# RWKV's output projection in a two-layer hybrid trunk: its first two tiles issued as a pair

## The chip, the core and the metric

The kernel runs on one core of one Trainium2 chip. The metric is the device time of one execution in microseconds (us). Before the change it is 2279.49 us, the median of 3 runs that lay between 2275.8 and 2281.12 us.

## What is computed

Each of two layers mixes 512 tokens of 1024 channels in two ways, gates both and adds them up; a feed-forward block (FFN) with a short convolution and a small gated embedding follow.

```python
y_att = sliding_window_attention(q, k, v, att_sinks) @ w_o_att
y_rw = rwkv7_time_mix(rw, ...) @ w_o_rw                      # the projection that the change touches
mixed = sigmoid(gate_a) * y_att + sigmoid(gate_b) * y_rw
x = x + rmsnorm(mixed @ w_out)
h = rmsnorm(x)
ua, ub = split(causal_dwconv3(h @ w_up))                     # 2816 + 2816 channels
x = x + rmsnorm((gelu(ua) * ub) @ w_down)
x = x + rmsnorm(sigmoid(x @ w_ple_gate) * (p[i] @ w_ple))
```

Everything is in 32-bit floats.

## The kernel before

**Layout.** Activations lie transposed: a tensor of 1024 channels is eight tiles of 128 channels x 512 tokens. A weight matrix is cut into output tiles `m` of 128 columns; each is loaded in two halves of four 128-row blocks (`w`, 128x512, 256 KB).

**A matmul in three.** To keep 32-bit accuracy, every operand is split in two parts: a rounded high part and the rest. ScalarE (ACT) writes the high part (`wh` of a weight, `yr` or `hh` of an activation), then VectorE (DVE) subtracts to get the low part (`wl`, `hl`; for `yr` both parts bear that name). `mm3` (lines 251 to 256) then issues three TensorE (PE) matmuls per block `k`: line 254 high x high, line 255 the low part of the activation, line 256 the low part of the weight. An output tile of 1024 input channels takes 8 x 3 = 24 matmuls.

**Accumulators (PSUM banks).** `PM(cls)` (line 102) hands out the bank in which an output tile is summed. There are two banks named `pm` and one named `pf`. With class "x" a counter `self.nx` goes round the three: m, m, f, m, m, f, ... (line 104). With class "m" or "f" the bank is named by the caller and the counter stays where it is. A bank is used again only when the instruction that reads its sum has finished; the scheduler puts a wait on the first matmul of the next tile in it.

**Weight buffers.** `load_w` (line 136) has classes too: "m" has 2 raw buffers `w` and 3 each of `wh` and `wl`; "f" has 1 and 2 and 2. Class "x" alternates between them by a counter of its own, `self.nw`; `proj` (line 258) loads an output tile's two halves so, one in each class, and issues its 24 matmuls.

**Who sets the order.** The kernel is written in program order, but a scheduler reorders each engine's instructions by priority and by its own idea of when operands are ready. Each engine then runs its list strictly in that order. All data transfers are issued by one queue (SP) in order too.

**Around the change.** The recurrence of RWKV runs in four groups (`rwkv`, line 572); group g writes rows 2g and 2g+1 of the scratch tensor `yrd`. The next work in the program is the gate of the RWKV branch (`gate`, line 835), the attention's output projection (`att_out`, line 510, weights `w_oa`, evacuated by DVE as `ta`), and then the part that the change edits (lines 921 to 942): eight loads `yr <- yrd` of 128x512, each split into the two parts; then for each of eight output tiles m a projection by `w_or[l, m]`, and its evacuation `tb <- tb, p` (which frees the bank), `+ mt`, and a split into `hh`, `hl`. The scratch buffers of `ta`, `yr`, `tb` and `mt` come from one pool of three (`F`, line 847), so that the fourth load of `yr` has to wait until an earlier buffer has been split.

**After it.** The same class "x" counter is used by the projections that come later: `w_out` (`lin`, line 949), the FFN's up projection (`ffn`, line 1096), its down projection and the embedding's gate. In between some tiles name their bank. In the FFN, `conv(m)` (line 1099) runs for the pairs (0, 22), (1, 23), (2, 24), (3, 25) and so on (FT = 22). The first five tiles were computed ahead; tile 3 is taken in bank `pf` and tile 24 in a bank `pm`, by name (line 1101); tile 25 is the first that takes a bank from the counter. What frees a bank here is DVE's `un <- p, rs` (line 1107), followed by two convolution steps `cv` (lines 1109, 1110).

Of the kernel before, what the change touches and what calls it, by code (L numbers as in the profile page):

```python
# [19 lines left out]
P = 128  # L20
T = 512
DM = 1024
KT = DM // P
# [32 lines left out]
class Trunk:  # L56
# [291 lines left out]
    @staticmethod  # L348
    def row(t, k):
        return t[k * P:(k + 1) * P, :]  # L350
# [491 lines left out]
    def run(self):  # L842
        nc, tc, a = self.nc, self.tc, self.a
# [22 lines left out]
        for l in range(self.L):  # L866
# [54 lines left out]
            yact = []  # L921
# [10 lines left out]
                yact.append(self.split(t, hi, lo))  # L932
            self.cls = "x"
            mixed = []
            for m in range(KT):
                ps = self.proj(a["w_or"][l, m], yact)
                tb, mt = F("tb"), F("mt")
                self.dma(tb, row(self.tbd, m))
                self.dma(mt, row(self.mad, m))
                self.stt(tb, tb, 1.0, ps, ALU.add, ALU.mult)  # L940
                self.tt(tb, tb, mt, ALU.add)
                mixed.append(self.split(tb, *hb[m]))
# [68 lines left out]
            for m in range(KT):  # L1011
# [3 lines left out]
                ps = self.PM("f") if m % 2 else self.PT("ple")  # L1015
# [189 lines left out]
```

## Time and profile before

| | us |
|---|---|
| three timed runs: median (lowest, highest) | 2279.49 (2275.8, 2281.12) |
| the profiled execution, own time | 2275.79 |
| its span, first to last instruction | 2274.1 |
| PE busy | 2192.8 (96% of the span) |
| DVE busy | 1544.7 (68%) |
| ACT busy | 1120.0 (49%) |
| mean granted TensorE clock | 0.993 |

The profile is of one execution. All places in time below are microseconds from the start of its span. A timeline row reads: start, duration, engine, line, operation, output <- inputs, shapes, count; in brackets the idle time of the engine before it and what ended that. A matmul's duration covers its way through the array; what a matmul costs in a stream is the distance from its start to the next one's start. Timeline rows leave out the buffer numbers, the rows of the program's order keep them.

### The profile page before, as it was taken

The numbers are of one execution on the slowest core, as the hardware profiler recorded it, in microseconds if no ns is written. First come the engines' busy times: TensorE is split into PE (matmuls) and PEld (weight loads), VectorE is DVE, ScalarE is ACT, GpSimd is POOL, SyncE is SP. The second block draws the span as 40 slices with busy tenths as digits, with TensorE's granted clock in tenths as the row PEclk, the third lists the DMA queues.
The fourth block names the chain that finished last, engine by engine and source line by source line (L and its number), as shares of the span: only waits on it lengthen the run. The fifth ranks groups of instructions, "written<-read, shape, count | busy, mean of one in ns | idle before, by whom it ended". The sixth has DMA issues, their size and how long they took to land. (4 is left out here: it accounts for less than half of the span.)

```text
span 2274.1 us, 39486 instructions
## 1 busy us (share of the span) xinstructions
PE 2192.8 (96%) x14340; PEld 1730.1 (76%) x14340; DVE 1544.7 (68%) x3683; ACT 1120.0 (49%) x2450; POOL 26.7 (1%) x86
## 2 busy tenths in 40 slices
PE   7999999999999999999999999999999999999996
PEld 6766776667689788888896677766677888888886
DVE  6864689777666877733877647789666668776356
ACT  4566445555444654432445655556443545454332
POOL 1000000000000000000000000000000000000000
PEclk9999999999999999999999999999999999999998
DMA  4522333355571433343235233333456623333431
GB/s 154 172 91 93 104 92 88 85 145 176 178 247 31 134 98 98 95 121 114 83 128 154 86 123 96 82 96 103 124 168 208 214 75 102 98 98 98 123 106 60
DMA packets 204515, 269.40 MB, mean 118 GB/s; under 512 B 71840, under 2 KB 84640, under 8 KB 204320
## 3 DMA queue, kind: packets, MB, share of 16 engines
q1 hardware_dynamic: 204320, 266.88, 38.7%
q8 instruction: 113, 1.85, 0.3%
q14 instruction: 82, 0.67, 0.1%
HBM read 218.95 MB, written 42.47 MB: 115 GB/s over the span
## 5 line engine op out<-in xcount | busy, mean ns | idle before, releaser
L125 ACT ACTIVATE wh<-w 128x512 fp32r<-128x512 f32 (+1 forms) x590 | 352.9, 605 | 514.5 <-PE pm L255 173.3
L159 DVE TENSOR_TENSOR wl<-w,wh 128x512 fp32r<-128x512 f32 (+2 forms) x574 | 376.7, 661 | 263.9 <-ACT wh L125 243.7
L254 PE MATMUL pm<-hh,wh 128*128 128x512 f32 x1040 | 421.1, 405 | 1.9 <-ACT wh L125 1.2
L256 PE MATMUL pm<-hh,wl 128*128 128x512 f32 x1040 | 419.4, 403 | 2.7 <-DVE wl L159 2.7
L255 PE MATMUL pm<-hl,wh 128*128 128x512 f32 x1040 | 415.3, 399 | 0.0
L254 PEld LDWEIGHTS pm<-hh,wh 128*128 128x128 f32 x1040 | 195.4, 188 | 51.3 <-issue 7.0
L256 PEld LDWEIGHTS pm<-hh,wl 128*128 128x128 f32 x1040 | 195.5, 188 | 48.4 <-DVE wl L159 4.3
L255 PEld LDWEIGHTS pm<-hl,wh 128*128 128x128 f32 x1040 | 195.3, 188 | 41.5 <-issue 2.4
L254 PE MATMUL pf<-hh,wh 128*128 128x512 f32 x512 | 205.5, 401 | 5.4 <-ACT hh L125 2.4
L256 PE MATMUL pf<-hh,wl 128*128 128x512 f32 x512 | 204.0, 398 | 0.0
L255 PE MATMUL pf<-hl,wh 128*128 128x512 f32 x512 | 203.2, 397 | 0.5 <-DVE hl L128 0.5
L134 DVE SCALAR_TENSOR_TENSOR cv<-un,vec,cv 128x510 f32<-128x510 f32 (+1 forms) x176 | 130.8, 749 | 23.2 <-ACT cv L125 20.6
L254 PEld LDWEIGHTS pf<-hh,wh 128*128 128x128 f32 x512 | 96.4, 188 | 33.9 <-ACT gt L125 4.8
L256 PEld LDWEIGHTS pf<-hh,wl 128*128 128x128 f32 x512 | 96.7, 189 | 23.3 <-issue 2.3
L255 PEld LDWEIGHTS pf<-hl,wh 128*128 128x128 f32 x512 | 96.7, 189 | 21.0 <-DVE hl L128 1.2
L254 PE MATMUL pm<-uh,wh 128*128 128x512 f32 (+1 forms) x248 | 89.3, 360 | 2.0 <-ACT wh L125 2.0
L256 PE MATMUL pm<-uh,wl 128*128 128x512 f32 (+1 forms) x248 | 89.4, 361 | 0.0
L255 PE MATMUL pm<-ul,wh 128*128 128x512 f32 (+1 forms) x248 | 88.9, 359 | 0.0
L125 ACT ACTIVATE cv<-un,vec 128x512 f32<-128x512 f32 x88 | 71.2, 814 | 28.3 <-DVE un L128 28.2
L128 DVE TENSOR_TENSOR acc<-acc,sq 128x256 f32<-128x256 f32 (+1 forms) x114 | 49.9, 462 | 38.5 <-ACT sq L125 38.0
L128 DVE TENSOR_TENSOR un<-pm,rs 128x512 f32<-128x512 f32 x56 | 38.5, 690 | 39.8 <-PE pm L256 39.8
L703 DVE TENSOR_TENSOR Z<-Z 128x126 f32<-128x126 f32 (+22 forms) x248 | 62.0, 250 | 3.7
(409 smaller groups left out, 4440.5 us busy)
## 6 DMA issues: line engine op xcount, KB each, us to landing
w<-in_w_up_dram SPq DMA_DIRECT2D x156, 256.0 KB
w<-in_w_dn_dram SPq DMA_DIRECT2D x80, 256.0 KB
w<-in_w_q_dram SPq DMA_DIRECT2D x32, 256.0 KB
w<-in_w_ga_dram SPq DMA_DIRECT2D x32, 256.0 KB
w<-in_w_k_dram SPq DMA_DIRECT2D x32, 256.0 KB
w<-in_w_r_dram SPq DMA_DIRECT2D x32, 256.0 KB
w<-in_w_v_dram SPq DMA_DIRECT2D x32, 256.0 KB
w<-in_w_gb_dram SPq DMA_DIRECT2D x32, 256.0 KB
```

The source lines that it names most:

```text
L125: return self.nc.scalar.activation(out=out, in_=in_, func=func, **kw)
L128: return self.nc.vector.tensor_tensor(out=out, in0=in0, in1=in1, op=op)
L134: return self.nc.vector.scalar_tensor_tensor(out=out, in0=in0, scalar=s, in1=in1, op0=op0, op1=op1)
L159: self.nc.vector.tensor_tensor(out=wl, in0=w, in1=wh.bitcast(F32), op=ALU.subtract)
L254: mm(ps, wh, ah, start=start, stop=False)
L255: mm(ps, wh, al, start=False, stop=False)
L256: return mm(ps, wl, ah, start=False, stop=stop).ins
L703: nc.vector.tensor_tensor(out=zt[:, :n, jj + 1:], in0=zt[:, :n, jj + 1:], in1=tv, op=ALU.add)
```

## The change

The first two output tiles of the projection, m = 0 and m = 1, are no longer done by `proj` one after the other. Tile 0 gets a bank `pm` and both its weight halves in class "m", tile 1 gets bank `pf` and both halves in class "f". Their matmuls are written as: blocks 0 to 5 of tile 0, blocks 0 to 5 of tile 1, then blocks 6 and 7 (the rows of the recurrence's last group) of tile 0 and of tile 1. The evacuations and tiles 2 to 7 are as before. Since the two tiles name their banks, the counter `nx` moves six steps in this loop, not eight; `nw` moves twelve, not sixteen.

```diff
             self.cls = "x"
             mixed = []
+            pair = [(self.PM(c), self.whole(a["w_or"][l, i], P, c)) for i, c in enumerate("mf")]
+
+            for ks in (range(6), range(6, KT)):
+                for ps, ws in pair:
+                    for k in ks:
+                        self.mm3(ps, ws[k], yact[k], k == 0, k == KT - 1)
             for m in range(KT):
-                ps = self.proj(a["w_or"][l, m], yact)
+                ps = pair[m][0] if m < 2 else self.proj(a["w_or"][l, m], yact)
                 tb, mt = F("tb"), F("mt")
                 self.dma(tb, row(self.tbd, m))
                 self.dma(mt, row(self.mad, m))
```

What the scheduler makes of it, at three places.

**PE, layer 0, the first matmuls of the projection.** `yr_6909`/`yr_6910` are the two parts of block 0, `yr_6915`/`yr_6916` those of block 1. Before, `pm_6953` is tile 0 and `pm_6998` tile 1:

```order
L254 MATMUL pm_6953<-yr_6909,wh_6956 128x512
L255 MATMUL pm_6953<-yr_6910,wh_6956 128x512
L256 MATMUL pm_6953<-yr_6909,wl_6958 128x512
L254 MATMUL pm_6953<-yr_6915,wh_6956 128x512
L254 MATMUL pm_6998<-yr_6909,wh_7001 128x512
L255 MATMUL pm_6998<-yr_6910,wh_7001 128x512
L256 MATMUL pm_6998<-yr_6909,wl_7003 128x512
L255 MATMUL pm_6953<-yr_6916,wh_6956 128x512
```

After, tile 1 is `pf_6966`:

```order
L254 MATMUL pm_6953<-yr_6909,wh_6956 128x512
L255 MATMUL pm_6953<-yr_6910,wh_6956 128x512
L256 MATMUL pm_6953<-yr_6909,wl_6958 128x512
L254 MATMUL pm_6953<-yr_6915,wh_6956 128x512
L254 MATMUL pf_6966<-yr_6909,wh_6969 128x512
L255 MATMUL pf_6966<-yr_6910,wh_6969 128x512
L256 MATMUL pf_6966<-yr_6909,wl_6971 128x512
L255 MATMUL pm_6953<-yr_6916,wh_6956 128x512
```

Nothing has moved: the scheduler interleaved tiles 0 and 1 already. Of the rest of the two tiles only two matmuls have moved: the second and third of tile 1's block 5 stand ahead of tile 0's block 6 now, no longer among its block 7. Tile 1's bank is another.

**PE, layer 0, the start of the FFN's up projection.** `pm_8470` is tile 24, `pf_8507` tile 3, and the last name tile 25, the first whose bank comes from the counter. Before:

```order
L255 MATMUL pm_8470<-hl_116,wh_8380 128x512
L256 MATMUL pm_8470<-hh_115,wl_8382 128x512
L256 MATMUL pf_8507<-hh_115,wl_8394 128x512
L254 MATMUL pm_8538<-hh_101,wh_8541 128x512
L255 MATMUL pm_8538<-hl_102,wh_8541 128x512
L256 MATMUL pm_8538<-hh_101,wl_8543 128x512
```

After:

```order
L255 MATMUL pm_8470<-hl_116,wh_8380 128x512
L256 MATMUL pm_8470<-hh_115,wl_8382 128x512
L256 MATMUL pf_8507<-hh_115,wl_8394 128x512
L254 MATMUL pf_8538<-hh_101,wh_8541 128x512
L255 MATMUL pf_8538<-hl_102,wh_8541 128x512
L256 MATMUL pf_8538<-hh_101,wl_8543 128x512
```

No row has moved. Tile 25 is in bank `pf` now, the one that the row just ahead of it has filled for tile 3. DVE's list, from the start of this FFN to `un <- pf_8507`, is the same in both kernels. In layer 1 the counter has been shifted twice, and tile 25 is in a bank `pm` before and after.

**SP, layer 1, the transfers around the load of block 1 (`yr_18754`).** `w_18858` and `w_18814` are the second half of tile 1's weights, `w_18975` a half of tile 4's, `mad` a store, `yr_18760` block 2. Before:

```order
L122 DMA yrd1_12444<-yo_18045 128x512
L122 DMA g_18058<-gd1_12879 128x512
L122 DMA mad1_18419<-ta_18666 128x512
L122 DMA yr_18754<-yrd1_12444 128x512
L122 DMA w_18858<-in_w_or_dram 128x512
L122 DMA w_18975<-in_w_or_dram 128x512
L122 DMA yrd1_12444<-yo_18059 128x512
L122 DMA yr_18760<-yrd1_12444 128x512
```

After:

```order
L122 DMA yrd1_12444<-yo_18045 128x512
L122 DMA g_18058<-gd1_12879 128x512
L122 DMA w_18814<-in_w_or_dram 128x512
L122 DMA mad1_18419<-ta_18666 128x512
L122 DMA yr_18754<-yrd1_12444 128x512
L122 DMA w_18975<-in_w_or_dram 128x512
L122 DMA yrd1_12444<-yo_18059 128x512
L122 DMA yr_18760<-yrd1_12444 128x512
```

The weight half has moved from two places behind the store to the place ahead of it, so that it is now ahead of block 1's load. ACT and DVE likewise split this weight half ahead of block 1, and no longer behind it. On PE in layer 1 four matmuls (block 0 of tile 1, and the first of tile 2) have moved ahead of the first one that needs block 1, and tile 3 has bank `pf`, which was tile 1's.

## The prediction

> **What bounds the kernel now.** I read the page's busy shares first, then PE's timeline where the edited projection runs, then every later place where the bank counter matters.
>
> ```profile
> span 2274.1 us, 39486 instructions
> PE 2192.8 (96%) x14340; PEld 1730.1 (76%) x14340; DVE 1544.7 (68%) x3683; ACT 1120.0 (49%) x2450; POOL 26.7 (1%) x86
> ```
>
> PE is the bound: it stands still for 81 us of 2274. An edit of order can win only out of those 81 us, and whatever makes PE wait at a place where it does not wait now is paid in full, as long as PE stays busy behind it. In the projection PE waits once in each layer. PE's timeline, layer 0 and then layer 1:
>
> ```profile
> 609.37 0.39 PE L256 MATMUL pm<-yr,wl 128*128 128x512 f32 x1
> 612.79 1.11 PE L254 MATMUL pm<-yr,wh 128*128 128x512 f32 x2 [3.03 <-ACT yr L125]
> ...
> 1730.49 0.39 PE L256 MATMUL pm<-yr,wl 128*128 128x512 f32 x1
> 1733.10 0.73 PE L254 MATMUL pm<-yr,wh 128*128 128x512 f32 x2 [2.23 <-ACT yr L125]
> ```
>
> The waits of 3.03 and 2.23 us are not for the last group's rows. In the order of the program the first instruction behind the 3.03 us wait needs block 3 and the one behind the 2.23 us wait needs block 1; both are rows of early groups, and what is late is their load and split. These places are all that the edit aims at. With the clock (below) they are worth at most 3.03 + 1.7 + 2.23 = 7 us.
>
> **The projection, layer 0: nothing to gain.** PE's list had the two tiles interleaved already, and SP's, ACT's and DVE's lists are the same up to block 4, weights by other names aside. So the 3.03 us wait for block 3 comes again. What can be new is that tile 1 now sums in bank `pf`, which the last tile of the attention's projection has just used. DVE's row that frees it, then PE's first rows that would need it:
>
> ```profile
> 605.42 0.69 DVE L134 SCALAR_TENSOR_TENSOR ta<-ta,pf 128x512 f32<-128x512 f32 x1 [0.29 <-PE pf L256]
> ...
> 606.04 0.72 PE L254 MATMUL pm<-yr,wh 128*128 128x512 f32 x2
> 606.61 0.40 PE L255 MATMUL pm<-yr,wh 128*128 128x512 f32 x1
> ```
>
> The bank is free at 605.42 + 0.69 = 606.11. The second of the two merged matmuls is tile 1's first, 0.23 ahead of 606.61, at 606.38: 0.27 us to spare. Were it late by some tenths, the wait for block 3 behind it would take that up. The weight splits that ACT and DVE have ahead of block 5 now are covered by PE's matmuls on blocks 3 and 4. Layer 0's projection: 0, bounds -0.2 and +0.5.
>
> **The FFN's start, layer 0: a new wait.** Tile 25 moves to bank `pf`, whose last matmul for tile 3 is the row just ahead of it. So PE cannot go on before DVE has run `un <- pf` for tile 3. PE's timeline there:
>
> ```profile
> 757.35 0.39 PE L256 MATMUL pf<-hh,wl 128*128 128x512 f32 x1
> 757.57 0.39 PE L254 MATMUL pm<-hh,wh 128*128 128x512 f32 x1
> 757.80 0.39 PE L255 MATMUL pm<-hl,wh 128*128 128x512 f32 x1
> 758.75 0.50 PE L256 MATMUL pm<-hh,wl 128*128 128x512 f32 x1 [0.56 <-DVE wl L159]
> 759.08 0.40 PE L254 MATMUL pm<-hh,wh 128*128 128x512 f32 x1
> ```
>
> And DVE's:
>
> ```profile
> 757.35 0.75 DVE L134 SCALAR_TENSOR_TENSOR cv<-un,vec,cv 128x510 f32<-128x510 f32 x1
> 758.01 0.69 DVE L159 TENSOR_TENSOR wl<-w,wh 128x512 fp32r<-128x512 f32 x1
> 758.61 0.68 DVE L128 TENSOR_TENSOR ul<-cv,uh 128x512 fp32r<-128x512 f32 x1
> 759.21 0.69 DVE L159 TENSOR_TENSOR wl<-w,wh 128x512 fp32r<-128x512 f32 x1
> 759.81 0.68 DVE L128 TENSOR_TENSOR un<-pm,rs 128x512 f32<-128x512 f32 x1
> 760.41 0.68 DVE L159 TENSOR_TENSOR wl<-w,wh 128x512 fp32r<-128x512 f32 x1
> 761.01 0.68 DVE L128 TENSOR_TENSOR un<-pf,rs 128x512 f32<-128x512 f32 x1
> ```
>
> Before, tile 25 starts at 757.57, stands 0.7 us for its low weight, and its fourth matmul is at 759.08. DVE has no idle in its rows: it is behind here, and its list is the same after the change, so `un <- pf` ends at 761.01 + 0.68 = 761.69 as before. From a DVE result to the PE matmul that waits for it, the rows give 758.75 - (758.01 + 0.69) = 0.05. Tile 25 starts at 761.74; the first matmul after a wait costs 0.33 (758.75 to 759.08), the next ones 0.23, so its fourth is at 761.74 + 0.33 + 2 x 0.23 = 762.53. **Delay: 762.53 - 759.08 = 3.45 us.** The 0.7 us wait for the low weight is inside it, since that is ready at 758.70. Bounds 3.0 and 3.8, if DVE runs half a step (0.6 us) earlier or later. The next tiles 4, 26 and 5 have banks that are free by then, and their weights are split by DVE ahead of or soon after this, so nothing is won back: PE has no wait over 0.5 us in the rest of this FFN.
>
> **The clock behind that wait.** PE's granted clock falls to a half for 3.41 us at a time. Five stretches of that length, from the answer by windows (from:to, length, PE busy and matmuls, weight loads, DVE, ACT, POOL, granted clock, DMA):
>
> ```profile
> 609.52:612.94 3.42, 0.39 (x3) 0.15 (x2) 1.56 (x3) 0.83 (x2) 0.00 (x0) 1.00 0.91 348
> 612.94:616.35 3.41, 3.41 (x9) 2.50 (x10) 2.36 (x4) 1.69 (x3) 0.00 (x0) 0.50 0.84 252
> 616.35:619.76 3.41, 3.41 (x17) 2.81 (x16) 1.92 (x4) 1.87 (x3) 0.00 (x0) 1.00 0.70 201
> 1210.27:1213.68 3.41, 1.99 (x7) 0.78 (x5) 3.36 (x8) 2.05 (x4) 0.00 (x0) 1.00 0.79 274
> 1213.68:1217.10 3.42, 3.26 (x8) 2.40 (x8) 3.33 (x9) 1.83 (x5) 0.00 (x0) 0.50 0.81 275
> 1729.09:1732.51 3.42, 1.79 (x8) 1.13 (x7) 1.98 (x3) 0.87 (x2) 0.00 (x0) 1.00 0.92 319
> 1732.51:1735.92 3.41, 2.82 (x12) 2.36 (x13) 1.38 (x2) 1.31 (x3) 0.00 (x0) 1.00 0.95 281
> ```
>
> A full stretch holds some 15 matmuls of 512 columns. Stretches with 3 and with 7 were followed by one at half clock, the stretch with 8 was not: the line lies near half. A slow stretch filled with work loses half of 3.41, 1.7 us. The new wait lasts from 757.57 to 761.74, 4.17 us, so at least one stretch is less than half filled, wherever the borders fall. How much is lost hangs on them: if the slow stretch lies partly on the wait itself, 0.5 to 1.3; one full stretch, 1.7; if that is thin too and a second one follows, up to 2.6. I take 1.6, near the middle and near the one full stretch that the 3.03 us wait cost.
>
> The Trainium skill (TensorE: Matmul & The Clock Gate, "Why this matters for your kernels") puts the line elsewhere: no PE gaps over some 3 us, since a whole idle window sends the clock back. This trace disagrees at 1213.68, where a stretch with 7 matmuls was enough; what a rule of whole stretches would give is the first rival.
>
> **The projection, layer 1: about nothing.** SP has the second half of tile 1's weights ahead of the load of block 1 now. ACT's rows for block 1, that weight, and block 2; PE's first matmul on block 2; and SP's issues:
>
> ```profile
> 1732.42 0.63 ACT L125 ACTIVATE yr<-yr 128x512 fp32r<-128x512 f32 x1 [2.09 <-DMA yr<-yrd]
> 1733.17 0.64 ACT L125 ACTIVATE wh<-w 128x512 fp32r<-128x512 f32 x1
> 1735.79 0.63 ACT L125 ACTIVATE yr<-yr 128x512 fp32r<-128x512 f32 x1 [1.98 <-DMA yr<-yrd]
> ...
> 1736.47 0.73 PE L254 MATMUL pm<-yr,wh 128*128 128x512 f32 x2
> ...
> 1728.12 0.38 SPq L122 DMA_DIRECT2D yr<-yrd  x1
> 1728.55 0.99 SPq L122 DMA_DIRECT2D w<-in_w_or_dram  x2
> ```
>
> Block 1 and this weight half change places in the queue, so block 1 should be ready when the weight was: some 0.7 us later (1733.17 against 1732.42). PE has four matmuls (0.9 us) more to do ahead of it, and ten instead of fourteen behind it until it needs block 2, which was ready at 1736.42 and was needed at 1736.47. So the same work is done when block 2 comes. Block 3 takes the buffer that block 1 frees, so its load may go out 0.7 us later: at most +0.7, below nothing not more than -0.2. Further on, tile 3 shares tile 1's bank, which by DVE's list is freed about when PE gets there: 0 to +0.5. I take +0.3 for layer 1, bounds -0.2 and +1.2; it is nearer to nothing since the load of block 2 is not moved.
>
> **Sum.** 0 + 3.45 + 1.6 + 0.3 = +5.35 us: 2275.79 + 5.35 = 2281.1 in the profiled execution's own time. That execution lies 3.7 us below the median of the runs, so the median comes to 2279.5 + 5.35 = **2284.8 us**, 0.23% slower. About 0.2% (4.6 us) is what a measurement of this kernel can tell from no change.
>
> **The rivals.**
>
> *The clock holds.* If only a stretch without any matmul lowers it, the 4.17 us wait covers a whole stretch in (4.17 - 3.41) / 3.41 = 22% of positions; in the others the sum is 3.45 + 0.3 = +3.75: 2283.2, within 0.2%. For it: the 2.23 us wait of layer 1 cost no clock. Against: 1213.68. Chance 0.14.
>
> *Not slower: the waits for `yr` are filled.* If the paired order lets the loads of the blocks come sooner (the weight halves of tile 1 in the other class leave SP's queue earlier), both waits go, -7, and the FFN's wait remains: 5.05 - 7 = -1.9: 2277.6. It decides in whether block 3 is split before 609.6 in layer 0, 3 us sooner than now. Against: SP's list up to that load is the same. Chance 0.06.
>
> *Next to nothing happens.* The scheduler had done the interleaving itself, and DVE frees `pf` in time. For that it would have to be 4.1 us ahead of these rows; it has no idle to draw that from. +0.3: 2279.8. Chance 0.10.
>
> *Slower still.* All upper bounds meet: 3.8 + 2.6 + 1.2 + 0.5 = +8.1: 2287.6. Chance 0.08.
>
> The forecast keeps 0.62.
>
> **How the numbers follow.** The forecast's own bounds run from 3.0 + 0.5 - 0.4 = +3.1 to +8.1; most of it lies between +4.3 and +6.5, and its share above 4.6 us I put at three quarters, the runs' own spread taken in. Slower: 0.62 x 0.75 + 0.08 + 0.14 x 0.25 = 0.58. Faster needs -4.6 us, which only the filled waits come near: 0.03. Within: 0.39. The range takes in the clock rival and "next to nothing" at its low end and the slower case with the spread of the runs (some 2 us about the median) at its high end; it leaves out the filled waits and the tails: 2279.3 to 2289.5.
>
> **What would show it.** In the changed profile: at about 757.6 PE stops for some 4 us, ended by DVE's `un` (helper line 128), and DVE's row `un <- pf` is the one that ends just ahead; one or two stretches of granted clock 0.50 at or after it; the same 3 us wait for `yr` at 609.6; in layer 1 the wait at 1730.5 in two pieces, with PE at block 2 by about 1736.5. The forecast is wrong if PE runs on through 757.6, if DVE frees the bank before 758, or if the wait at 609.6 is under 2 us.

## The result, and the profile after

| | before | after |
|---|---|---|
| median of the timed runs, same chip (us) | 2278.64 (6 runs, 2275.80 to 2281.12) | 2285.33 (6 runs, 2284.69 to 2289.15) |
| after / before, 95% interval | | 1.0032 (1.0021 to 1.0042) |
| the profiled execution, own time / span | 2275.79 / 2274.1 | 2285.38 / 2283.7 |

The change costs 6.7 us by the medians, 0.3%. (The ratios leave out the one slow execution, 7317.56 us, which experiment 3 below had among its 12 runs.) The page of the changed kernel, its span and PE's share:

```profile
span 2283.7 us, 39487 instructions
PE 2195.2 (96%) x14340; PEld 1732.1 (76%) x14340; DVE 1546.1 (68%) x3683; ACT 1120.7 (49%) x2450; POOL 26.6 (1%) x86
```

The same 14340 matmuls are busy 2.4 us longer, and PE stands still for 88.5 us instead of 81.3. The first place that was forecast is the start of layer 0's FFN. PE's timeline there (start, duration; in brackets the idle time ahead and what ended it):

```profile
759.21 0.39 PE L256 MATMUL pf<-hh,wl 128*128 128x512 f32 x1
763.68 0.77 PE L254 MATMUL pf<-hh,wh 128*128 128x512 f32 x1 [4.09 <-DVE un L128]
764.25 0.63 PE L255 MATMUL pf<-hl,wh 128*128 128x512 f32 x1
764.67 0.63 PE L256 MATMUL pf<-hh,wl 128*128 128x512 f32 x1
765.10 0.63 PE L254 MATMUL pf<-hh,wh 128*128 128x512 f32 x1
```

And DVE's:

```profile
761.66 0.68 DVE L128 TENSOR_TENSOR un<-pm,rs 128x512 f32<-128x512 f32 x1
762.26 0.68 DVE L159 TENSOR_TENSOR wl<-w,wh 128x512 fp32r<-128x512 f32 x1
762.86 0.68 DVE L128 TENSOR_TENSOR un<-pf,rs 128x512 f32<-128x512 f32 x1
```

Tile 25, in `pf` now, stands 4.09 us until DVE has read tile 3 out of that bank (762.86 + 0.68 = 763.54). Before, the row ahead started at 757.35 and tile 25's fourth matmul at 759.08, 1.73 later; now it is 765.10 - 759.21 = 5.89. That is 4.16 us already, and the matmuls behind the wait follow each other every 0.43 us, not every 0.23. The windows say why. From:to, length, PE busy, weight loads, DVE, ACT, POOL, granted clock, DMA share, GB/s, first at the FFN, then at the wait for `yr` in layer 0's projection:

```profile
759.01:762.42 3.41, 0.59 (x3) 0.17 (x1) 3.41 (x7) 1.31 (x3) 0.00 (x0) 1.00 0.20 59
762.42:765.83 3.41, 2.15 (x5) 1.80 (x6) 3.41 (x6) 2.72 (x4) 0.00 (x0) 0.50 0.62 178
765.83:769.25 3.42, 3.42 (x9) 2.68 (x9) 2.75 (x5) 1.76 (x3) 0.00 (x0) 0.50 0.27 82
769.25:772.66 3.41, 3.41 (x16) 2.76 (x16) 1.28 (x2) 0.77 (x2) 0.00 (x0) 1.00 0.43 146
608.78:612.19 3.41, 1.48 (x7) 0.87 (x5) 1.06 (x2) 0.65 (x1) 0.00 (x0) 1.00 0.93 339
612.19:615.61 3.42, 1.99 (x5) 1.57 (x6) 1.67 (x3) 1.56 (x3) 0.00 (x0) 0.51 0.69 225
615.61:619.02 3.41, 3.41 (x10) 2.67 (x9) 1.78 (x3) 2.52 (x5) 0.00 (x0) 0.50 0.65 219
```

At both places the stretch that holds most of the wait is followed by two at half clock, since the wait's end (1.26 us and 1.43 us of it) lies in the first of them. Set against the kernel before, the same matmul in order of execution lies 1.84 us later at 739 us and 8.01 us later at 833 us: the difference, 6.17 us, is the FFN's whole loss. The rest of PE's waits in the two projections, in the changed kernel:

```profile
609.87 0.40 PE L256 MATMUL pf<-yr,wl 128*128 128x512 f32 x1
613.62 0.80 PE L254 MATMUL pm<-yr,wh 128*128 128x512 f32 x1 [3.36 <-ACT yr L125]
...
1742.93 0.47 PE L254 MATMUL pm<-yr,wh 128*128 128x512 f32 x1 [1.82 <-ACT wh L125]
1744.04 0.50 PE L254 MATMUL pm<-yr,wh 128*128 128x512 f32 x1 [0.64 <-ACT yr L125]
1746.97 0.50 PE L254 MATMUL pm<-yr,wh 128*128 128x512 f32 x1 [0.34 <-ACT yr L125]
1749.30 0.50 PE L254 MATMUL pm<-yr,wh 128*128 128x512 f32 x1 [0.41 <-ACT yr L125]
```

Layer 0 waits 3.36 us for block 3, as before (3.03). In layer 1 the wait of 2.23 us has become several. The profile puts the first of them down to a weight split on ACT. The rows of ACT and DVE that matter here; the last is the split of block 1:

```profile
1736.84 0.63 ACT L125 ACTIVATE wh<-w 128x512 fp32r<-128x512 f32 x1 [0.80 <-PE pm L255]
...
1742.10 0.68 DVE L134 SCALAR_TENSOR_TENSOR ta<-ta,pm 128x512 f32<-128x512 f32 x1
1742.17 0.63 ACT L125 ACTIVATE wh<-w 128x512 fp32r<-128x512 f32 x1 [2.17 <-DMA w<-in_w_or_dram]
...
1743.35 0.63 ACT L125 ACTIVATE yr<-yr 128x512 fp32r<-128x512 f32 x1 [0.55 <-DMA yr<-yrd]
```

By the order of the program the matmul that stands there is the first of tile 2. Its own weights are split by ACT's row at 1736.84 and had long been ready; the row at 1742.17 is the second half of tile 1's weights, which this matmul does not read. What it waited for is its bank: the attention's last tile lay in that `pm` until DVE's `ta <- ta, pm` ended at 1742.78. (In experiment 7, which has the same banks here, the profile names that row itself, for a wait of 0.60 us.) The wait is hidden by the one behind it, since block 1 was ready only at 1743.98. By the same count of matmuls this projection costs 1.0 us more.

The other differences, +0.6 us by 600 us, ahead of the edited projection, +1.2 in layer 0's projection (one stretch at half clock more than before) and +0.9 in layer 0's down projection, belong to the two executions and not to the change: experiment 2, where both projections are those of the kernel before, has +1.2 and +1.1 us at the same two places. So of the 9.6 us between the two profiled executions some 3 are chance: before's lies 2.9 us under its median, after's on it.

### The profile page after: what moved, and what is told of

Its sections match the earlier page's. It is cut to its first block, busy times and chain, and to the rows that moved or that the text cites. A ratio compares the mean times of both kernels' runs of the same rounds, so it can differ in the third digit from the quotient of the medians.

```text
span 2283.7 us, 39487 instructions
## 1 busy us (share of the span) xinstructions
PE 2195.2 (96%) x14340; PEld 1732.1 (76%) x14340; DVE 1546.1 (68%) x3683; ACT 1120.7 (49%) x2450; POOL 26.6 (1%) x86
## 5 line engine op out<-in xcount | busy, mean ns | idle before, releaser
L254 PE MATMUL pm<-uh,wh 128*128 128x512 f32 (+1 forms) x256 | 96.0, 375 | 1.6 <-ACT wh L125 1.6
L255 PE MATMUL pm<-ul,wh 128*128 128x512 f32 (+1 forms) x256 | 95.9, 375 | 0.0
L256 PE MATMUL pm<-uh,wl 128*128 128x512 f32 (+1 forms) x256 | 95.9, 374 | 0.0
```

The lines of the kernel that those rows point to most:

```text
L254: mm(ps, wh, ah, start=start, stop=False)
L255: mm(ps, wh, al, start=False, stop=False)
L256: return mm(ps, wl, ah, start=False, stop=stop).ins
```

## The experiments

The theory after the result: tile 25's bank costs it all, wait and clock; the pair as such costs next to nothing. The rival: the pair costs, by its waits and weights in the projections. Each kernel ran 11 or 12 times, beside 23 to 35 runs of the kernel before on the same chip.

**1. Only tile 25's bank, taken out of the change.**

```diff
+                ps = None
+                if (l, m) == (0, FT + 3):
+                    self.nx = (self.nx + 1) % 3
+                    ps = self.PM("m")
-                ps = self.proj(a["w_up"][l, m], h, key=m)
+                ps = self.proj(a["w_up"][l, m], h, key=m, ps=ps)
```

> The changed kernel with one bank altered: tile 25 of layer 0's FFN is summed in a bank pm by name; the counter is still stepped there, so every other tile has its bank as in the changed kernel. Theory (the bank of tile 25 is what costs): PE goes on behind tile 3 without the 4.09 us wait and without half clock; the time falls by 5 to 6 us against the changed kernel, to within 1.5 us of the kernel before. Rival (the pair and the shifted banks elsewhere cost it: 0.3 us more wait on yr in layer 0, a second half-clock stretch there, 0.9 us in the down projection): the FFN's wait goes, but at least 3 us of the 6.7 remain.

Measured: 2279.89 against 2279.49 us, 1.0003 (0.9989 to 1.0017). PE's timeline at the place:

```profile
757.87 0.39 PE L256 MATMUL pf<-hh,wl 128*128 128x512 f32 x1
758.09 0.39 PE L254 MATMUL pm<-hh,wh 128*128 128x512 f32 x1
758.32 0.39 PE L255 MATMUL pm<-hl,wh 128*128 128x512 f32 x1
759.18 0.50 PE L256 MATMUL pm<-hh,wl 128*128 128x512 f32 x1 [0.47 <-DVE wl L159]
```

PE goes on at once, only the old short wait for the low weight is left. One accumulator of one tile takes away the loss as far as the runs can tell, with the pair and every other shifted bank still there.

**2. Only tile 25's bank, put into the kernel before.** Tiles 25 and 4 change banks, so that the rest stays.

```diff
+                ps = None
+                if l == 0 and m in (FT + 3, 4):
+                    self.nx = (self.nx + 1) % 3
+                    ps = self.PM("mf"[m > FT])
-                ps = self.proj(a["w_up"][l, m], h, key=m)
+                ps = self.proj(a["w_up"][l, m], h, key=m, ps=ps)
```

> The kernel before, no pair, with tiles 25 and 4 of layer 0's FFN changing banks: 25 in pf behind tile 3, 4 in pm. All other banks as before. Theory: PE waits some 4.1 us for DVE's un of tile 3 and half clock follows: 5 to 6 us slower than before, as the changed kernel or 1 us under it. Rival (pair): the wait appears but less than 3.5 us is lost in all, because the work behind catches up.

Measured: 2283.85 against 2279.49 us, 1.0028 (1.0015 to 1.0041): 6.4 us by the ratio, 4.4 by the medians. PE's timeline:

```profile
756.93 0.39 PE L256 MATMUL pf<-hh,wl 128*128 128x512 f32 x1
761.44 0.77 PE L254 MATMUL pf<-hh,wh 128*128 128x512 f32 x1 [4.12 <-DVE un L128]
762.01 0.63 PE L255 MATMUL pf<-hl,wh 128*128 128x512 f32 x1
```

The wait and the half clock of the changed kernel, without any pair.

**3. The pair, with the counter put right behind it.**

```diff
+            self.nx = (self.nx + 2) % 3
             for m in range(KT):
                 ps = pair[m][0] if m < 2 else self.proj(a["w_or"][l, m], yact)
```

> The changed kernel with the counter moved on two steps right behind the pair, so that from tile 2 of the projection on every tile has its bank as in the kernel before; tile 2 then stands in pf right behind tile 1. Theory: no FFN wait, the pair itself costs nothing that can be told: -0.5 to +1.5 us against before, the upper end if tile 2 waits for tile 1's bank. Rival (the pair costs): +3 us or more.

Measured: 2284.33 against 2279.49 us, 1.0020 (1.0010 to 1.0029). A miss: +4.6 us by the ratio, as the rival had it, though the FFN's wait is gone. The trace shows another one. PE's timeline in layer 1, and below it DVE's:

```profile
1739.47 0.39 PE L256 MATMUL pm<-yr,wl 128*128 128x512 f32 x1
1742.00 0.55 PE L254 MATMUL pf<-yr,wh 128*128 128x512 f32 x1 [2.13 <-DVE ta L134]
```

```profile
1741.26 0.68 DVE L134 SCALAR_TENSOR_TENSOR ta<-ta,pf 128x512 f32<-128x512 f32 x1
```

Here it is tile 1 of the pair that finds its bank taken: `pf` holds the last tile of the attention's projection, which DVE has not read yet. In the changed kernel the shifted counter had put that tile in a `pm`. And tile 2, in `pf` too, can no longer be interleaved with tile 1. By the same count of matmuls the projection of layer 1 costs 1.8 us against before; other losses in this execution are stretches at half clock (2.4 us in layer 0's projection, 3.0 at 1600 us), so where the 4.6 us of the runs lie is not shown. Experiment 5 tells whether this is the pair or its banks.

**4. The counter shifted, without the pair.**

```diff
                 mixed.append(self.split(tb, *hb[m]))
+            self.nx = (self.nx + 1) % 3
```

> The kernel before, no pair, with the counter moved on one step behind the projection in each layer: the same phase of the banks from there on as the changed kernel has. Theory: all of the loss is here, +5 to +7 us against before, with the wait of 4 us behind tile 3 in layer 0. Rival (pair): under +3 us.

Measured: 2283.36 against 2279.49 us, 1.0015 (1.0005 to 1.0025): +3.4 us, the interval 1.1 to 5.7. PE's timeline in layer 0's FFN:

```profile
754.21 0.39 PE L256 MATMUL pf<-hh,wl 128*128 128x512 f32 x1
758.70 0.77 PE L254 MATMUL pf<-hh,wh 128*128 128x512 f32 x1 [4.10 <-DVE un L128]
```

The place is the same and costs 5.8 us in this trace; the total is less than the +5 to +7 us that I expected, though its interval overlaps that of the changed kernel. The profiled execution lies 3.5 us under the median of its runs: in it PE came to layer 0's projection 1.4 us earlier, waited 2.00 us there and kept its clock. Whether the rest of the gap is chance or something that the pair adds, this run alone leaves open.

**5. The pair by itself.** Tiles 0 and 1 as in the change, weights in both classes, but with the banks of the kernel before.

```diff
-            pair = [(self.PM(c), self.whole(a["w_or"][l, i], P, c)) for i, c in enumerate("mf")]
+            pair = [(self.PM("x"), self.whole(a["w_or"][l, i], P, c)) for i, c in enumerate("mf")]
```

> The pair by itself: tiles 0 and 1 are written as in the changed kernel, with their weights in the classes m and f, but their banks come from the counter as in the kernel before, so that every bank in the program is the one of the kernel before. Theory (the bank phase is what costs, the pair next to nothing): -0.5 to +1.5 us against before; layer 0's projection as before, layer 1's up to 1 us longer because the weight half stands ahead of block 1. Rival (the pair itself costs, as the restored-counter kernel's +4.5 us would have it): +3 us or more.

Measured: 2278.55 against 2278.46 us, 1.0001 (0.9990 to 1.0012). PE's timeline, the waits of layer 0's and layer 1's projection:

```profile
611.99 0.73 PE L254 MATMUL pm<-yr,wh 128*128 128x512 f32 x2 [2.07 <-ACT yr L125]
...
1736.73 0.73 PE L254 MATMUL pm<-yr,wh 128*128 128x512 f32 x2 [0.87 <-ACT yr L125]
1739.89 0.74 PE L254 MATMUL pm<-yr,wh 128*128 128x512 f32 x2 [0.53 <-ACT yr L125]
1742.47 0.73 PE L254 MATMUL pm<-yr,wh 128*128 128x512 f32 x2 [0.67 <-ACT yr L125]
```

The pair alone costs or gains nothing that can be told, the interval being -2.3 to +2.7 us: layer 1's wait is in three pieces of 2.07 us together, against 2.23. In the source this kernel and number 3 differ in tile 1's bank alone, so the 4.6 us there come from that bank and the order of the next tiles that the scheduler makes of it. The rival falls.

**6. Block 3 loaded early, no pair.** `WA` is a pool whose four buffers are idle by then.

```diff
-                t = F("yr")
+                t = (WA if j == 3 else F)("yr")
```

> The kernel before with one buffer changed: block 3 of yr is loaded into a buffer that is idle by then, instead of waiting for one of the pool of three. Nothing is paired. Theory (the projection's waits are for the loads of early blocks, not for the last group's rows): the 3.03 us wait in layer 0 falls under 1.5 us and layer 1's 2.23 us stays or moves to another block: 1 to 4 us faster than before. Rival (the wait moves on to block 4 or 2): within 1 us of before.

Measured: 2277.38 against 2278.46 us, 1.0000 (0.9989 to 1.0010). PE's timeline, in layer 0's projection and in the down projection:

```profile
607.86 0.73 PE L254 MATMUL pm<-yr,wh 128*128 128x512 f32 x2 [0.31 <-ACT yr L125]
609.49 0.51 PE L255 MATMUL pm<-yr,wh 128*128 128x512 f32 x1 [0.67 <-DVE yr L128]
617.00 0.73 PE L254 MATMUL pm<-yr,wh 128*128 128x512 f32 x2 [0.50 <-ACT yr L125]
...
1032.62 0.50 PE L254 MATMUL pm<-uh,wh 128*128 128x512 f32 x1 [1.36 <-ACT wh L125]
1070.69 0.39 PE L254 MATMUL pm<-uh,wh 128*128 128x256 f32 x1 [1.82 <-ACT wh L125]
```

The wait was for block 3, as the theory says: it is gone, and the half clock behind it too, 2.4 us in the trace. Yet the gain of 1 to 4 us that I expected does not show; the interval, -2.5 to +2.3 us, just takes in the 2.4 us. In this execution 1.2 of them are lost again by 1090 us, where PE waits longer for weights (before: 1.25 and 0.50 us), and the other 1.2, by 1146 us, in a second stretch at half clock behind the 5.00 us wait between the FFN and the embedding's gate. That the early load brings this about is not shown: the wait at 1070 us lies between 0.26 and 1.77 us in the other ten changed kernels, and is 1.61 us in experiment 2, which moves no load. The same with blocks 1 and 3 early:

> The kernel before with only the two late blocks, 1 and 3, loaded into idle buffers. Theory (these two waits are all that the projection loses): both fall under 1 us, and 1 to 4 us are won. Rival (what is won here is waited for again at the down projection, where the weights come as fast as the queue brings them, as with block 3 alone): within 1.5 us of before, with longer waits for wh at 1030 and 1070 us.

2276.75 against 2277.14 us, 1.0000 (0.9989 to 1.0010): no gain that can be told here either. Layer 0's wait fell to 0.37 us, layer 1's only broke up (1.54, 0.39 and 0.79).

**7. A shorter wait in the changed kernel.** Tiles 24 and 3 swap banks in layer 0; DVE's `un` of tile 24 stands two rows ahead of that of tile 3.

```diff
-                ps = self.PM("fm"[m > FT])
+                ps = self.PM("fm"[(m > FT) == (l > 0)])
```

> The changed kernel with the banks of tiles 24 and 3 swapped in layer 0: tile 25 is then behind DVE's un of tile 24, two DVE rows (1.2 us) earlier than that of tile 3. Theory (the wait's length is the loss, the clock comes on top): PE waits some 2.9 us instead of 4.1, with one stretch of half clock, not two: the FFN's start loses 3.4 to 4.9 us instead of 6.1, and the median lies 1 to 3 us under the changed kernel. Rival (clock needs a whole stretch without work): no stretch of half clock, 2.4 us lost. Rival (the wait is for something else than the bank): no change against the changed kernel.

Measured: 2280.61 against 2278.46 us, 1.0016 (1.0002 to 1.0030), by the ratios 3.6 us under the changed kernel, with intervals that overlap. PE's timeline, and the windows around it:

```profile
758.43 0.39 PE L256 MATMUL pm<-hh,wl 128*128 128x512 f32 x1
761.75 0.47 PE L254 MATMUL pf<-hh,wh 128*128 128x512 f32 x1 [2.94 <-DVE un L128]
...
762.51 0.39 PE L254 MATMUL pf<-hh,wh 128*128 128x512 f32 x1
```

```profile
757.05:760.46 3.41, 1.76 (x8) 1.13 (x6) 3.41 (x7) 1.55 (x3) 0.00 (x0) 1.00 0.00 0
760.46:763.88 3.42, 2.13 (x10) 1.80 (x11) 3.42 (x6) 2.14 (x4) 0.00 (x0) 1.00 0.61 196
```

The wait is 2.94 us, as expected from two DVE rows less, so it is the bank. In this execution a border of the stretches cuts it nearly in half, 1.76 and 2.13 us of work remain in them, and the clock holds: the loss is the bare delay, (762.51 - 758.43) - 1.73 = 2.35 us, less than the 3.4 to 4.9 that I expected with one slow stretch. It is the fastest of the kernel's 12 runs, 2.8 us under their median, so it does not show what the others lose. The 2.35 us are the number of the rival for which only an empty stretch lowers the clock; but this rival does not survive the changed kernel's 608.78, where 1.48 us of work were not enough.

**8. Four early blocks, without and with the pair.** Blocks 0 to 3 in idle buffers; then the same in the kernel of experiment 5.

```diff
-                t = F("yr")
+                t = (WA if j < 4 else F)("yr")
```

> The kernel before with blocks 0 to 3 of yr loaded into idle buffers, so that none of them waits for the pool of three. Theory (loads of early blocks are what PE waits for): both projection waits fall under 1 us and the stretch of half clock behind the first goes too: 3 to 6 us faster than before. Rival: the earlier loads move the splits in among the recurrence's work on ACT and DVE and cost there what they save here: within 2 us of before or slower.

Without the pair: 2276.82 against 2278.46 us, 0.9992 (0.9982 to 1.0002), which can't be told from no change; I had expected 3 to 6 us. Of the two waits only layer 0's, 1.15 us now, came near what I expected.

> The pair with the banks of the counter, and blocks 0 to 3 of yr loaded into idle buffers: the two edits that cost nothing or gained, together. Theory (once the early blocks are there in time, the last group's rows could be what PE waits for, and the pair puts them at the end): 1 to 4 us faster than before and up to 2 us faster than the four early blocks without the pair. Rival (the scheduler had interleaved the two tiles already, so the pair adds nothing): as the four early blocks alone, 0 to 3 us faster than before.

With it: 2273.07 against 2277.14 us, 0.9981 (0.9971 to 0.9991), 4.3 us faster than before by the ratio and the fastest kernel here. PE's timeline has one wait left in layer 0 and none over 0.3 us in layer 1:

```profile
618.23 0.50 PE L254 MATMUL pm<-yr,wh 128*128 128x512 f32 x1 [1.13 <-ACT yr L125]
```

The intervals of the two overlap, so that the pair adds something here is likely by the trace (layer 1 lost 1.74 us to block loads without it) and not shown.

## Why the prediction was right, and where it was not

- **Layer 0's projection, 0 (-0.2 to +0.5): right.** The wait for block 3 came again, 3.36 us, and lay between 2.00 and 3.40 in the other kernels that load it late, paired or not. The +1.2 us of the profiled execution are a second stretch at half clock, as in experiment 2 without the pair; experiment 5, with it, loses 0.8 us less here than the kernel before.
- **The FFN's new wait, +3.45 (3.0 to 3.8): right.** At full clock the fourth matmul would have come 0.33 + 2 x 0.23 = 0.79 behind 763.68, at 764.47: 764.47 - 759.21 - 1.73 = 3.53 us. Experiments 1 and 2 show the bank of tile 25 as the cause from both sides.
- **The clock, +1.6 (0.5 to 2.6): the mis-sized term.** It measured 6.17 - 3.53 = 2.6 us, my upper bound. The step that failed is "if the slow stretch lies partly on the wait itself, 0.5 to 1.3": I took a thin slow stretch as a small loss, and a second one behind it as the far end. It is the dear case: a stretch at half clock with 2.15 us of work was followed by another, and that one was full. All three kernels with the 4.1 us wait had two slow stretches behind it; the place cost 6.2 us in experiment 2 and 5.8 in experiment 4.
- **Layer 1's projection, +0.3 (-0.2 to +1.2): within its bounds,** +1.0 in the profiled execution. I expected block 1 some 0.7 us later; behind the projection's first matmul it was ready after 3.01 us before and 4.40 now. In three more executions with the same order of transfers, of experiments 1, 7 and 5, it was ready after 3.83, 2.80 and 2.67 us, and the projection cost +0.8, -0.3 and -0.4 us. So the loss goes with the coming of block 1, which differs between executions, and is not settled to better than a microsecond. That tile 2 meets a taken bank I had not seen; under the wait for block 1 it cost nothing.
- **The sum, +5.35, against +6.7 by the medians:** 1.0 of the missing 1.3 us is the clock. The predicted time, 2284.8 us, lies 0.5 us from the median measured, in part by luck: it started from a median of 2279.49 us, which six runs put 0.85 us lower.
- **The rivals.** "The clock holds" came out in experiment 7 alone, where a border halved the wait. "The waits for `yr` are filled" fell with experiment 5: with the pair alone both waits stay, 2.07 us each. What shortens layer 0's wait is an early load of the blocks; that the kernel gains by it is shown only together with the pair, in experiment 8. "Next to nothing happens" fell with the 4.09 us wait. Of "slower still" only the clock's upper bound was reached.

The Trainium skill (Perfetto Trace Analysis, "Matmuls") asks for independent groups of matmuls in different PSUM banks, so that the evacuation of one runs under the next. The traces agree and add the price of one neighbour that doesn't: 4.1 us of wait, since DVE was two tiles behind.

## What to carry to other kernels

A counter that hands out accumulators is part of the schedule of everything behind it: before an edit makes it skip a step, list which bank each later tile gets, and look for a tile that directly follows its bank's last user, above all where tiles with banks named by hand meet tiles of the counter. To learn what a local edit is worth, hold the counter's phase, or the shift is measured instead. And before work is reordered around a wait, look up which operand ends it: here it was the load of an early block, which no order of the last group's rows can shorten. The name that the profile gives to the end of a wait is a first guess: compare it with the operands and the bank of the matmul that stood.

## What the runs showed of the hardware

**How full a stretch must be.** In twelve traces (both kernels and the ten experiments), from 100 to 2250 us, I sorted the stretches of 3.41 us by PE's busy time. Of those at full clock with at most 1.7 us, 27 of 28 were followed by half clock; with 1.7 to 2.1 us, 16 of 47; with more, 3 of some 7400. A stretch at half clock went on into another in 14 of 14 cases under 2.6 us, and in 2 of 48 above. So in this kernel the clock falls behind some 1.7 us of standstill in one stretch, at times behind 1.3, and a wait that reaches into the slow stretch and leaves it less than 2.6 us of work costs another one. The busy time in the profile is not all that counts: two of the three falls behind fuller stretches came in the recurrence, behind 3.2 us of busy PE with 64 matmuls of 32x32 in it. The Trainium skill (TensorE: Matmul & The Clock Gate, "Why this matters for your kernels") names one idle window; these traces show half of one.

**Chance in equal kernels.** The borders of the stretches lie elsewhere in each execution: the slow stretch in layer 0's projection began at 612.9 us before, 612.2 after, 613.7 in experiment 5. The Trainium skill (TensorE: Matmul & The Clock Gate, "What's actually happening") has a free-running window of 3413 ns, which agrees. So each wait of some 2 to 3 us is a draw for a loss of some 1.7 us, half of a stretch, and the mean granted clock goes with the time: 35 runs of the kernel before, beside experiments 1 to 4, went from 2273.05 us at 0.994 to 2288.71 us at 0.987. At the same mean clock of 0.991 the kernel before took 2280.6 us (9 runs), the changed one 2285.2 (2 runs) and experiment 1 2279.8 (3 runs). The 4.6 us between the first two are of the size of the bank's bare delay of 3.5 us, as far as two runs and a clock rounded to 0.001 can tell.
